# Gates of two of three branches moved from small tiles into halves of weight tiles during the up products of a gated three-branch layer

## The chip, the cores and the metric

One core of a Trainium2 chip runs the whole layer as one program. The metric is the device time of that program in microseconds, the median of three runs. Besides TensorE (PE in the profile) the core has VectorE (DVE), ScalarE (ACT), GpSimd (POOL) and SyncE (SP). In this kernel SP issues almost all transfers from its instruction stream, in order; POOL issues the transfers that add to what is already in a tile.

## The reference, cut to what matters

The input x is 512 tokens by 2048 channels, one layer, all in fp32. What the change touches is the last third of the layer:

```python
hn = rmsnorm(x, norm_g)
proj = einsum('bsd,dc->bsc', hn, w_in)
gates = sigmoid(proj[..., QKVG_COLS + N_HEADS:] + b_gate).reshape(b, s, 3, 2048)
# ya, yb, yc: three attention branches over proj, 4 heads of 128 each
ys = stack([from_heads(ya), from_heads(yb), from_heads(yc)], axis=2)
ys = ys * silu(br[:, :, :, 3])
up = einsum('bsnw,nwd->bsnd', ys, w_up)        # 3 branches, 512 -> 2048
merged = sum(gates * up, axis=2)
return x + einsum('bsd,de->bse', merged, w_out)
```

## The kernel before

**Arithmetic.** Every fp32 product is made of three reduced-precision matmuls: each operand is split into a high and a low half. A weight tile arrives as `raw` (128x1024 fp32, 512 KB, 8 tiles, `NR`); ACT copies it to `wh` (`prep`, L409, 3 buffers), DVE subtracts to get `wl` (L419, 2 buffers), and from then on the raw tile is free. PE runs the products of one such tile, a *unit*, at L277. The input projection and the output product use a seven-product scheme of block sums, for which some `w_out` and `w_in` tiles are first added to each other in DRAM-to-SBUF transfers that POOL issues (`add_up`, L320).

**Stages.** First the input projection and the attention heads (to about 980 us), then the up products, then the output product. The up products go through 12 pairs (g, b): g is one of four quarters of the 2048 output channels, b the branch (0 is C, 1 is B, 2 is A). Their order is `UPS`: (0,0) (0,1) (2,0) (2,1) (0,2) (2,2) (1,0) (1,1) (1,2) (3,0) (3,1) (3,2). A pair has two units of 24 matmuls, and in the second of them its four blocks of 128 tokens (tb) end one after the other. A tile of the output product serves 12 matmuls; the first eight `w_out` tiles are loaded while up products run, and four of them get another tile added first. The attention products of the last A head (L1111 to L1113) stand in the middle of this stage.

**Gates.** The gate logits were stored to DRAM earlier (`gl`). For each (g, b, tb), `gates_of` takes one 128x512 tile of the pool `t2` (20 tiles, `NT`; 3 of them, `KEPT`, are held back from tasks with slack), reads the logits into it (SP, L293, `sg<-gl`), and ACT makes the sigmoid (L1305). `taken` in `up_units` then empties PSUM: DVE multiplies the block by the gate (L1321) and, for b of 1 and 2, adds it to the sum of the branches before it (L1328). After that the tile of b = 1, 2 goes back to `t2`; that of b = 0 holds the sum.

**Merged sums.** When the third branch of a quarter is done, the sum must be turned, channels to partitions. Quarters 0 and 2 go through DRAM: a 32x32 transpose on DVE (L1354), a store, four transposing reads (`back`, L312). Quarters 1 and 3 are turned on PE (`spun_m`, L1385) and copied out by ACT (L1392). Each turned block becomes a *first half* (quarters 0 and 1: one DVE subtraction at L1401, one split at L258 and L262) or a *second half* (quarters 2 and 3: three DVE operations of 128x256 at L268, and three splits).

**What sets the order.** The program is written out by a planner (`Flow`) that keeps a clock for each engine and takes, from the tasks that can start earliest on an engine, the one with the smallest due time: its ready time plus its slack (`MAS` for first halves, `MBS` for second halves), or an explicit one. A task asks the pools (`Slots`) for tiles and waits, in the plan, until one is free. On the chip every engine then follows its written list. A load that stands in SP's list ahead of others holds them up until its own tile is free. Weight loads are issued by one task (`loads`), in the order of the units, as soon as a raw tile is free; gate reads are listed three or two units ahead of the pair's first unit.

Of the kernel before, what the change touches and what calls it, by code (L numbers as in the profile page):

```python
# [21 lines left out]
NB = 3  # L22
# [5 lines left out]
NQ = 4  # L28
# [7 lines left out]
A, B, C = 0, 1, 2  # L36
# [28 lines left out]
class Flow:  # L65
# [16 lines left out]
    def give(self, slots, n=1):  # L82
        slots.free += [self.fin] * n
# [6 lines left out]
    def advance(self, task):  # L90
        while True:
            self.ready = task.ready
            w = task.wait
            if w is None:
                w = next(task.gen, None)
                if w is None:
                    self.tasks.remove(task)
                    task.engine = None
                    return
            task.wait = w  # L100
            if isinstance(w, Event):
                if w.t is None:
                    return
                task.ready = max(task.ready, w.t)
            elif callable(w):
                if not w():
                    return
            elif isinstance(w[0], Slots):
                slots, n = w
                more = n + (slots.kept if task.slack > 1 else 0)  # L110
                if len(slots.free) < more:
                    return
                slots.free.sort()
                due = max(task.ready, slots.free[more - 1])
                if due > self.now + EARLY:
                    task.until = due
                    return
                task.ready = max(task.ready, slots.free[n - 1])
                del slots.free[:n]
            else:  # L120
                task.engine, task.cost = w[:2]
                if task.engine != task.prev:
                    task.ready = max(task.ready, task.fin)
                    if task.engine == PE:
                        task.ready += MARGIN
                task.due = w[2] if len(w) > 2 else task.ready + task.slack
                return
            task.wait = None
# [47 lines left out]
def hybrid_kernel(  # L176
# [30 lines left out]
    flow = Flow()  # L207
# [4 lines left out]
    def t2(s, dt=F32):  # L212
        return tp.tile([P, S], dt, tag="t2", name=nm(s))
# [77 lines left out]
    def fetch(to, src, kb, run=2048):  # L291
        yield issue(0.37)
        nc.sync.dma_start(to, src)  # L293
        return Event(landing(flow.fin, kb, run))
# [82 lines left out]
    def at(u, g, slack=5.0):  # L377
        side.setdefault(u, []).append((g, slack))
# [379 lines left out]
    gl = {}  # L758
# [535 lines left out]

    sig, sig_ev = {}, {}

    def gates_of(n, g, tb):
        if (g, (C, B, A).index(n)) not in UPS[:EARLYG]:
            yield last_head.event("hl", 2)
        yield t2s, 1  # L1300
        t = sig[n, g, tb] = t2("sg")
        yield (yield from fetch(t, gl[n, g, tb], 256))
        yield last_head.event("g")
        yield ACT, act_us(S) + 0.1
        nc.scalar.activation(t, t, AF.Sigmoid)  # L1305
        set_(sig_ev[n, g, tb])

    merged, merged_ev = {}, {}

    def up_units(g, b):  # L1310
        n = (C, B, A)[b]
        ps = [None] * QB
        for tb in range(QB):
            sig_ev[n, g, tb] = Event()
            merged_ev[b, g, tb] = Event()

        def taken(tb):
            yield sig_ev[n, g, tb]
            t = sig[n, g, tb]
            yield DVE, dve_us(S)  # L1320
            nc.vector.tensor_mul(t, ps[tb], t)  # L1321
            give(accs)
            if b == 0:
                merged[g, tb] = t
            else:
                yield merged_ev[b - 1, g, tb]
                yield DVE, dve_us(S)
                nc.vector.tensor_add(merged[g, tb], merged[g, tb], t)  # L1328
                give(t2s)
            set_(merged_ev[b, g, tb])  # L1330

        def mms(i):
            def block(k, tb):
                y = b * NH + 2 * i + k
                return ys[y] and (*ys[y].block(tb), y_ev[y])

            def go(u):
                yield from products(u, ps, (0, 1), range(QB), block, i == 0, i == 1, None if i else (accs, acc),
                                    done=taken, outer=True)
            return go  # L1340

        return [Unit(mms(i), srcs=[w_up[g, b, i]]) for i in range(2)]
# [18 lines left out]
    def turned_m(g, i):  # L1361
        for tb in range(QB):
            yield md_ev[g, tb]
        yield t2s, 1
        m = t2("m")
        ev = yield from back(m, md[g][:, :, blk(i)])
        yield Event(ev.t + MEXTRA)
        arrived(g, i, m)
# [9 lines left out]
    def spun_m(g, i):  # L1378
        for tb in range(QB):
            yield merged_ev[NB - 1, g, tb]  # L1380
        yield atts, 1
        yield PE, 0.11 * QB
        ps = att()
        for tb in range(QB):
            nc.tensor.transpose(ps[:, blk(tb)], merged[g, tb][:, blk(i)], identf)  # L1385
        turns[g] = turns.get(g, 0) + 1
        if turns[g] == QB:
            give(t2s, QB)
        yield t2s, 1
        yield ACT, act_us(S)  # L1390
        m = t2("m")
        nc.scalar.activation(m, ps, AF.Copy)  # L1392
        give(atts)
        arrived(g, i, m)
# [11 lines left out]
    def merged_b(k, b):  # L1406
        a = kept_m[k]
        yield m1_ev[k]
        yield t2s, 1
        t = t2("mt")  # L1410
        if k % 2 == 0:
            yield t2s, 1
            mus[k // 2] = t2("mu")
        u = mus[k // 2][:, RH if k % 2 else LH]
        q = DVE, dve_us(HS)
        yield q
        minus(t[:, LH], b[:, RH], a[:, RH])
        yield q
        minus(t[:, RH], t[:, LH], a[:, LH])
        give(t2s)  # L1420
        yield q
        minus(u, t[:, LH], b[:, LH])
        yield xps, 1
        ev = Event()
        m23[k] = Parts("m23", [ev, ev])
        yield from split(m23[k].hi, m23[k].lo, two(t), S, ev)
        give(t2s)
        if k % 2 == 0:
            yield xps, 1
            m4[k // 2] = Parts("m4")  # L1430
            set_(m4_ev[k // 2])
        yield xps, 1
        ev = Event()
        m2[k] = Parts("m2", [ev, ev])
        yield from split(m2[k].hi, m2[k].lo, two(b), S, ev)
        give(t2s)
        yield m4_ev[k // 2]
        h, lo, ev = m4[k // 2].half(k % 2)
        yield from split(h, lo, u, HS, ev)
        if k % 2:  # L1440
            give(t2s)

    for g, b in UPS:
        for tb in range(QB):
            at(len(units) - (3 - tb // 2 if g or b else 2), lambda n=(C, B, A)[b], g=g, tb=tb: gates_of(n, g, tb))
        units.extend(up_units(g, b))
        if b < NB - 1:
            continue
        for i in range(QB):
            if g in DRAMS:  # L1450
                at(len(units) - 1, lambda g=g, i=i: folded(g, i))
                at(len(units) - 1 + MSKIP, lambda g=g, i=i: turned_m(g, i))
            else:
                at(len(units) - 1, lambda g=g, i=i: spun_m(g, i))
# [34 lines left out]
    def loads():  # L1489
        def x(kt):  # L1490
            yield t2s, 1
            if kt == 0:
                xraw[0], x_in[0].t = x_first, 3.6
                return
            xraw[kt] = t2("x")
            x_in[kt].t = (yield from fetch(xraw[kt], xT[kt], 256)).t

        def n(i):
            n_in[i].t = (yield from fetch(xnat[i // 2][:, i % 2, :], xn[i // NQ, i % NQ], 256)).t

        order = [("x", 0), ("w", 0), ("x", 1), ("w", 1), ("x", 2), ("x", 3), ("w", 2)] + [("n", i) for i in range(4)]
        order += [("x", 4), ("x", 5), ("w", 3)] + [("n", i) for i in range(4, 8)]
        order += [("x", 6), ("x", 7), ("w", 4)] + [("n", i) for i in range(8, 12)]
        order += [("x", 8), ("x", 9), ("w", 5)] + [("n", i) for i in range(12, 14)]
        for i in range(6, 9):
            order += [("x", 2 * i - 2), ("x", 2 * i - 1), ("w", i)] + [("n", j) for j in (14, 15) if i == 7]
        for kind, i in order:
            if kind == "x":
                yield from x(i)
            elif kind == "n":  # L1510
                yield from n(i)
            else:
                yield from units[i].load()
        for u in units[9:]:
            yield from u.load()

    for u, v in zip(units, units[1:]):
# [45 lines left out]
HSLACK = 12.0  # L1563
ENDSLACK, ENDOFF = 3.0, 3
EARLYG = 1
MEXTRA = 4.0
MAS = 1.0
MBS = 3.0

_OUT = (QB, NQ, P, S)  # L1570

# [45 lines left out]
```

## Time and profile before

| | |
|---|---|
| median of 3 runs | 1292.18 us (1288.53 to 1295.38) |
| the profiled execution | 1284.99 us |
| its span (first to last instruction) | 1283.3 us |
| what lies around the span | 1.7 us |
| PE busy | 1272.8 us, 99% of the span |
| DVE busy | 996.6 us, 78% |
| ACT busy | 754.6 us, 59% |
| POOL busy | 91.5 us, 7% |

Times inside the trace count from the start of the span. Three kinds of rows are used below. A row of a timeline has the start, the duration and the number of instructions that were run back to back, and in square brackets the idle time of the engine before it with what ended that. A row of the table by windows has, for each stretch, the busy time of PE, PEld, DVE, ACT and POOL with instruction counts, the granted clock of PE and the busy share and rate of the transfers. A row of the waits has an engine and line, what it waited for, and the total, the number and the longest.

### The profile page before, as it was taken

What the parts mean: (1) busy time and instruction counts of PE and PEld (TensorE: products, weight loads), DVE (VectorE), ACT (ScalarE), POOL (GpSimd) and SP (SyncE); (2) the same over time, 40 slices, a digit from 0 to 9 for tenths busy, and PEclk for the clock granted to TensorE, in tenths of its full rate; (3) what the DMA queues carried; (4) which work ended last, traced back from release to release, by engine and by line L of the source; (5) the groups of instructions that cost most, each with busy time, mean ns of one, the idle gap of its engine ahead of it and who ended that gap; (6) DMA issues with size and microseconds to landing.
All of it is one profiled execution on the core that took longest, in us unless ns stands there. A gap on an engine that the chain in (4) does not pass through costs nothing.

```text
span 1283.3 us, 17347 instructions
## 1 busy us (share of the span) xinstructions
PE 1272.8 (99%) x5716; PEld 1050.5 (82%) x5716; DVE 996.6 (78%) x1398; ACT 754.6 (59%) x1243; POOL 91.5 (7%) x115
## 2 busy tenths in 40 slices
PE   9999999999999999999999999999999999899998
PEld 7788888888888888888888888888887788788887
DVE  6948896987969677697776967769789587897665
ACT  7836566645856667566675666756657543664442
POOL 0001000110110101011011110101100000010100
PEclk9999999999999999999999999999999999999999
DMA  9685799987889878898788987889979979747863
GB/s 357 208 210 123 202 230 225 257 221 200 229 199 252 215 214 235 201 258 215 208 235 202 258 214 208 235 201 260 224 207 350 271 243 212 234 83 236 236 171 129
DMA packets 260666, 284.42 MB, mean 222 GB/s; under 512 B 169808, under 2 KB 180560, under 8 KB 260576
## 3 DMA queue, kind: packets, MB, share of 16 engines
q1 hardware_dynamic: 243152, 224.32, 58.4%
q0 software_dynamic: 14976, 54.53, 22.8%
q10 hardware_dynamic: 2448, 4.46, 0.9%
q8 instruction: 45, 0.74, 0.2%
q14 instruction: 45, 0.37, 0.1%
HBM read 240.73 MB, written 42.51 MB: 221 GB/s over the span
## 4 chain that ended last, share of the span: by engine, by line
PE 91%; DMA 5%; DVE 3%; SPq 1%; issue 1%; ACT 0%; DVEq 0%; ACTq 0%; POOLq 0%
PE acc L277 87%; DMA sg<-gl 1%; DMA raw<-in_w_col 1%; DMA al<-pd 1%; DVE wl L419 1%; PE att L273 1%; PE att L274 1%; PE att L272 1%; PE att L1113 1%; PE att L1112 1%; PE att L1111 1%; DMA raw<-in_w_up 1%; DVE m L262 1%; DMA gl<-v 0%; SPq L293 0%
## 5 line engine op out<-in xcount | busy, mean ns | idle before, releaser
L419 DVE TENSOR_TENSOR wl<-raw,wh 128x1024 fp32r<-128x1024 f32 (+1 forms) x405 | 492.5, 1217 | 227.5 <-PE acc L277 137.3
L409 ACT ACTIVATE wh<-raw 128x1024 fp32r<-128x1024 f32 (+1 forms) x404 | 426.0, 1056 | 354.7 <-PE acc L277 313.3
L277 PE MATMUL acc<-wh,x 128*128 128x512 f32 x1664 | 423.9, 390 | 0.0
L277 PEld LDWEIGHTS acc<-wh,x 128*128 128x128 f32 x1664 | 311.9, 188 | 68.1 <-issue 3.4
L277 PE MATMUL acc<-wh,t 128*128 128x512 f32 x1056 | 275.1, 390 | 0.0
L277 PE MATMUL acc<-wl,x 128*128 128x512 f32 x832 | 232.3, 390 | 0.8 <-DVE wl L419 0.8
L277 PEld LDWEIGHTS acc<-wh,t 128*128 128x128 f32 x1056 | 197.4, 188 | 40.0
L277 PEld LDWEIGHTS acc<-wl,x 128*128 128x128 f32 x832 | 155.7, 188 | 33.6 <-DVE wl L419 1.7
L277 PE MATMUL acc<-wl,t 128*128 128x512 f32 x528 | 154.4, 391 | 0.1
L320 POOL DMA_DIRECT2D raw<-in_w_col x88 | 76.1, 864 | 843.3 <-DMA raw<-in_w_col 228.6
L630 DVE TENSOR_TENSOR raw<-raw,raw 128x1024 f32<-128x1024 f32 x104 | 126.7, 1218 | 0.1
L277 PEld LDWEIGHTS acc<-wl,t 128*128 128x128 f32 x528 | 98.2, 188 | 20.9 <-DVE wl L419 1.2
L277 PE MATMUL acc<-wh,m 128*128 128x512 f32 x448 | 114.5, 389 | 0.0
L277 PE MATMUL acc<-wh,y 128*128 128x512 f32 x384 | 104.3, 393 | 2.2 <-DVE sg L1321 2.2
L277 PEld LDWEIGHTS acc<-wh,m 128*128 128x128 f32 x448 | 84.0, 188 | 17.5
L277 PEld LDWEIGHTS acc<-wh,y 128*128 128x128 f32 x384 | 72.5, 189 | 17.7 <-DVE sg L1321 2.6
L277 PE MATMUL acc<-wl,m 128*128 128x512 f32 x224 | 63.6, 390 | 0.2 <-DVE wl L419 0.2
L277 PE MATMUL acc<-wl,y 128*128 128x512 f32 x192 | 60.6, 395 | 0.0
L714 ACT ACTIVATE u<-acc 128x512 f32<-128x512 f32 x52 | 31.1, 598 | 41.4 <-PE acc L277 40.2
L277 PEld LDWEIGHTS acc<-wl,m 128*128 128x128 f32 x224 | 41.9, 188 | 9.2 <-DVE wl L419 0.6
L1321 DVE TENSOR_TENSOR sg<-acc,sg 128x512 f32<-128x512 f32 x48 | 32.7, 687 | 13.1 <-ACT sg L1305 8.3
L1305 ACT ACTIVATE sg<-sg 128x512 f32<-128x512 f32 x48 | 28.1, 621 | 24.7 <-DMA sg<-gl 24.6
(155 smaller groups left out, 960.9 us busy)
## 6 DMA issues: line engine op xcount, KB each, us to landing
raw<-in_w_col SPq DMA_DIRECT2D x191, 512.0 KB, 4.9
raw<-in_w_col POOLq DMA_DIRECT2D x88, 512.0 KB, 8.2
raw<-in_w_out SPq DMA_DIRECT2D x32, 512.0 KB, 4.0
raw<-in_w_up SPq DMA_DIRECT2D x24, 512.0 KB, 5.7
sg<-gl SPq DMA_DIRECT2D x48, 256.0 KB, 4.9
gl<-u SPq DMA_DIRECT2D x44, 256.0 KB, 4.7
raw<-in_w_out POOLq DMA_DIRECT2D x16, 512.0 KB, 6.3
qkl<-qd SPq DMA_DIRECT2D x96, 64.0 KB, 4.1
```

The costliest lines, as they stand in the source:

```text
L262: nc.vector.tensor_sub(lo, src, f(hi))
L272: nc.tensor.matmul(ps, lh, rh, start=start, stop=False, skip_group_check=more)
L273: nc.tensor.matmul(ps, lh, rl, start=False, stop=False, skip_group_check=more)
L274: nc.tensor.matmul(ps, ll, rh, start=False, stop=stop, skip_group_check=more)
L277: nc.tensor.matmul(ps, w, x, start=start, stop=stop, skip_group_check=more)
L320: nc.gpsimd.dma_start(to, src, accum_op=ALU.add)
L409: nc.scalar.activation(u.hi, u.raw, AF.Copy)
L419: nc.vector.tensor_sub(u.lo, u.raw, f(u.hi))
L630: nc.vector.tensor_add(to.raw, to.raw, self.raw)
L714: nc.scalar.activation(t, w, AF.Copy)
L1305: nc.scalar.activation(t, t, AF.Sigmoid)
L1321: nc.vector.tensor_mul(t, ps[tb], t)
```

## The change

**Gates of branches 1 and 2 no longer use `t2`.** A new pool `pairs` is filled with four of the eight raw tiles (`NPAIR`) at the point in `loads` where the first up unit's weight would be loaded. Two token blocks of a gate share one such tile, one half each; when both blocks have been added to the sum, the tile returns to `pairs`, and the last four go back to the weights. Between these points four raw tiles are left for `w_up` and for the first `w_out` tiles. Gates of branch 0 still take `t2` tiles, and the tiles of the merged sums (`m`, `mt`, `mu`) may now use the three that were held back.

**Order.** Gate reads are listed one unit earlier (`GAHEAD`), the plan counts each gate's data as there 4 us later (`GEXTRA`), the transposing reads 7 instead of 4 us later (`MEXTRA`), and first and second halves have slacks of 4 and 10 us instead of 1 and 3 (`MAS`, `MBS`). The lines after the new code move: L1305 is L1317, L1321 is L1346, L1328 is L1353, L1354 is L1379, L1385 is L1410, L1392 is L1417 and L1401 is L1426.

No matrix product, sigmoid, multiplication or transfer is added or left out. All four compute lists are the same up to about the end of the attention heads.

The core of the diff:

```diff
-                more = n + (slots.kept if task.slack > 1 else 0)
+                more = n + (slots.kept if task.slack > 1 and len(w) < 3 else 0)
...
+    pairs = Slots(0)
+
     def gates_of(n, g, tb):
         if (g, (C, B, A).index(n)) not in UPS[:EARLYG]:
             yield last_head.event("hl", 2)
-        yield t2s, 1
-        t = sig[n, g, tb] = t2("sg")
-        yield (yield from fetch(t, gl[n, g, tb], 256))
+        if n == C:
+            yield t2s, 1
+            t = sig[n, g, tb] = t2("sg")
+        else:
+            if tb % 2 == 0:
+                yield pairs, 1
+                both = raw_tile()
+                sig[n, g, tb], sig[n, g, tb + 1] = both[:, 0, :], both[:, 1, :]
+                set_(pair_ev[n, g, tb // 2])
+            yield pair_ev[n, g, tb // 2]
+            t = sig[n, g, tb]
+        ev = yield from fetch(t, gl[n, g, tb], 256)
+        yield Event(ev.t + GEXTRA)
         yield last_head.event("g")
         yield ACT, act_us(S) + 0.1
         nc.scalar.activation(t, t, AF.Sigmoid)
         set_(sig_ev[n, g, tb])
...
+    def pair_used(n, g, h):
+        pair_n[n, g, h] = pair_n.get((n, g, h), 0) + 1
+        if pair_n[n, g, h] == 2:
+            give(pairs)
+            pair_n["all"] = pair_n.get("all", 0) + 1
+            if pair_n["all"] > 2 * NQ * (NB - 1) - NPAIR:
+                pairs.free.sort()
+                raws.free.append(pairs.free.pop())
...
                 nc.vector.tensor_add(merged[g, tb], merged[g, tb], t)
-                give(t2s)
+                pair_used(n, g, tb // 2)
...
-        yield t2s, 1
+        yield t2s, 1, True
         m = t2("m")
...
-            at(len(units) - (3 - tb // 2 if g or b else 2), lambda n=(C, B, A)[b], g=g, tb=tb: gates_of(n, g, tb))
+            at(len(units) - (3 - tb // 2 + GAHEAD if g or b else 2), lambda n=(C, B, A)[b], g=g, tb=tb: gates_of(n, g, tb))
...
-        for u in units[9:]:
+        for i, u in enumerate(units[9:]):
+            if i + 9 == end:
+                yield raws, NPAIR
+                pairs.free += [max(flow.ready, flow.now)] * NPAIR
             yield from u.load()
...
-MEXTRA = 4.0
-MAS = 1.0
-MBS = 3.0
+MEXTRA = 7.0
+MAS = 4.0
+MBS = 10.0
+GEXTRA = 4.0
+GAHEAD = 1
+NPAIR = 4
```

Below, `order` rows show a stretch of one engine's list: the line, the instruction, the tile written and the tiles read, each with the number of its allocation, and the shape. First SP's list where the last gates of quarter 3 and the first `w_out` tiles are read, before (the logits `gl` numbered 3676 to 3840 are those of branch 0, 6519 to 6677 of branch 1):

```order
L293 DMA raw_9781<-in_w_out 128x1024
L293 DMA sg_9792<-gl_3698 128x512
L293 DMA sg_9807<-gl_3821 128x512
L293 DMA raw_9860<-in_w_out 128x1024
L293 DMA raw_9892<-in_w_out 128x1024
L293 DMA sg_9899<-gl_3840 128x512
L293 DMA raw_9942<-in_w_out 128x1024
L293 DMA sg_10008<-gl_6519 128x512
L293 DMA sg_10009<-gl_6541 128x512
L293 DMA raw_10017<-in_w_out 128x1024
```

and in the changed kernel (8937 to 8863 are of branch 2):

```order
L293 DMA raw_9712<-gl_6519 128x512
L293 DMA raw_9712<-gl_6541 128x512
L293 DMA raw_9734<-in_w_up 128x1024
```

with, eight transposing reads further down:

```order
L293 DMA raw_9771<-in_w_up 128x1024
L293 DMA raw_9760<-gl_6654 128x512
L293 DMA raw_9760<-gl_6677 128x512
L293 DMA raw_9805<-gl_8937 128x512
L293 DMA raw_9805<-gl_8944 128x512
L293 DMA raw_9829<-in_w_up 128x1024
L293 DMA raw_9881<-gl_8857 128x512
L293 DMA raw_9881<-gl_8863 128x512
L293 DMA raw_9897<-in_w_out 128x1024
L293 DMA raw_9964<-in_w_out 128x1024
```

Before, loads of `w_out` stood between the gate reads; now every gate read stands ahead of the first of them, with loads of `w_up` between.

Second, DVE's list at the end of pair (3,1), whose PSUM blocks are emptied by the rows with `acc`, before:

```order
L1401 TENSOR_TENSOR m_10040<-m_10040 128x256
L262 TENSOR_TENSOR m_1753_10044<-m_10034,m_1753_10044 128x2x256
L268 SCALAR_TENSOR_TENSOR mt_10010<-mt_10010,m_9570 128x256
L262 TENSOR_TENSOR m_1755_10056<-m_10040,m_1755_10056 128x2x256
L262 TENSOR_TENSOR m_1721_9915<-mu_9869,m_1721_9915 128x256
L419 TENSOR_TENSOR wl_10060<-raw_9646,wh_9987 128x1024
L262 TENSOR_TENSOR m_1742_9994<-mu_9946,m_1742_9994 128x256
L1321 TENSOR_TENSOR sg_10008<-acc_9925,sg_10008 128x512
L268 SCALAR_TENSOR_TENSOR mu_9946<-mt_10010,m_9737 128x256
L1321 TENSOR_TENSOR sg_10009<-acc_9938,sg_10009 128x512
L1328 TENSOR_TENSOR sg_9675<-sg_9675,sg_10008 128x512
L1328 TENSOR_TENSOR sg_9792<-sg_9792,sg_10009 128x512
```

and now:

```order
L419 TENSOR_TENSOR wl_9995<-raw_9771,wh_9939 128x1024
L1346 TENSOR_TENSOR raw_9712<-acc_9940,raw_9712 128x512
L1353 TENSOR_TENSOR sg_9613<-sg_9613,raw_9712 128x512
L1346 TENSOR_TENSOR raw_9712<-acc_9956,raw_9712 128x512
L1353 TENSOR_TENSOR sg_9614<-sg_9614,raw_9712 128x512
L1346 TENSOR_TENSOR raw_9760<-acc_9967,raw_9760 128x512
L1353 TENSOR_TENSOR sg_9660<-sg_9660,raw_9760 128x512
L268 SCALAR_TENSOR_TENSOR mt_9951<-mt_9951,m_9554 128x256
L1346 TENSOR_TENSOR raw_9760<-acc_9978,raw_9760 128x512
L1353 TENSOR_TENSOR sg_9661<-sg_9661,raw_9760 128x512
```

The first emptying of this pair stood behind first and second halves (L1401, L268, L262) of the merged sums; now it stands behind the weight's low half, and the four follow each other with one operation of a second half between.

Third, ACT's list near the start of the up products, where the four gates of pair (0,1) are made. The weights there are those of the sixth (`wh_9098`) and the seventh up unit (`wh_9137`), and the gates are the four after and around them, before:

```order
L409 ACTIVATE wh_9098<-raw_8863 128x1024
L1305 ACTIVATE sg_9018<-sg_9018 128x512
L1305 ACTIVATE sg_9026<-sg_9026 128x512
L1305 ACTIVATE sg_9045<-sg_9045 128x512
L409 ACTIVATE wh_9137<-raw_8897 128x1024
L1305 ACTIVATE sg_9064<-sg_9064 128x512
```

and now, where `wh_9094` is the sixth unit's and `wh_9132` the seventh's:

```order
L1317 ACTIVATE sg_8904<-sg_8904 128x512
L1317 ACTIVATE sg_8913<-sg_8913 128x512
L1317 ACTIVATE sg_8919<-sg_8919 128x512
L409 ACTIVATE wh_9094<-raw_8957 128x1024
L409 ACTIVATE wh_9132<-raw_9014 128x1024
L1317 ACTIVATE raw_8990<-raw_8990 128x512 x2
L1317 ACTIVATE raw_8991<-raw_8991 128x512 x2
```

Three of the four gates stood behind the sixth unit's weight and one behind the seventh's; now all four stand behind the seventh's.

More of the change, by code (lines that the diff above doesn't have):

```diff
@@ L108, in advance @@
             elif isinstance(w[0], Slots):
-                slots, n = w
-                more = n + (slots.kept if task.slack > 1 else 0)
+                slots, n = w[:2]
+                more = n + (slots.kept if task.slack > 1 and len(w) < 3 else 0)
                 if len(slots.free) < more:
@@ L1306, in gates_of @@
         set_(sig_ev[n, g, tb])
+    pair_ev, pair_n = {}, {}
+    def pair_used(n, g, h):
[6 more added lines that the diff above has]
+                raws.free.append(pairs.free.pop())
     merged, merged_ev = {}, {}
@@ L1312, in up_units @@
         ps = [None] * QB
+        for h in range(2):
+            pair_ev[n, g, h] = Event()
         for tb in range(QB):
@@ L1388, in spun_m @@
             give(t2s, QB)
-        yield t2s, 1
+        yield t2s, 1, True
         yield ACT, act_us(S)
@@ L1408, in merged_b @@
         yield m1_ev[k]
-        yield t2s, 1
+        yield t2s, 1, True
         t = t2("mt")
         if k % 2 == 0:
-            yield t2s, 1
+            yield t2s, 1, True
             mus[k // 2] = t2("mu")
```

## The prediction, made before the changed kernel was run

> **What bounds the kernel now.** I read the page first: the busy shares, the chain, the costliest groups.
>
> ```profile
> span 1283.3 us, 17347 instructions
> PE 1272.8 (99%) x5716; PEld 1050.5 (82%) x5716; DVE 996.6 (78%) x1398; ACT 754.6 (59%) x1243; POOL 91.5 (7%) x115
> L409 ACT ACTIVATE wh<-raw 128x1024 fp32r<-128x1024 f32 (+1 forms) x404 | 426.0, 1056 | 354.7 <-PE acc L277 313.3
> L419 DVE TENSOR_TENSOR wl<-raw,wh 128x1024 fp32r<-128x1024 f32 (+1 forms) x405 | 492.5, 1217 | 227.5 <-PE acc L277 137.3
> L1321 DVE TENSOR_TENSOR sg<-acc,sg 128x512 f32<-128x512 f32 x48 | 32.7, 687 | 13.1 <-ACT sg L1305 8.3
> L1305 ACT ACTIVATE sg<-sg 128x512 f32<-128x512 f32 x48 | 28.1, 621 | 24.7 <-DMA sg<-gl 24.6
> ```
>
> PE is the bound. It is outside its 1272.8 busy microseconds for 10.5 us in all, and the change adds or removes no matmul, so it can win only time that PE loses in the up products, and lose what it breaks there. So the second view is the table by windows of ten microseconds through that stage, and the third the waits of PE.
>
> ```profile
> 1000.00:1010.00 10.00, 10.00 (x46) 8.28 (x45) 6.54 (x10) 3.67 (x6) 0.00 (x0) 1.00 0.86 234
> 1010.00:1020.00 10.00, 9.18 (x43) 7.18 (x42) 6.78 (x12) 6.07 (x11) 0.00 (x0) 1.00 1.00 369
> 1100.00:1110.00 10.00, 8.48 (x41) 6.50 (x40) 10.00 (x21) 7.59 (x15) 1.72 (x2) 1.00 0.72 192
> 1110.00:1120.00 10.00, 7.78 (x27) 5.97 (x26) 10.00 (x19) 6.74 (x12) 0.00 (x0) 0.83 0.93 283
> ```
> ```profile
> PE acc L277 <- DVE sg L1321: 2.2, 1, 2.2
> PE att L1385 <- ACT m L1392: 1.5, 2, 1.0
> ```
>
> In an ordinary window PE is busy for all 10 us (second column). Three windows are not: one near 1010 and the last two of the stage, where DVE is busy for every microsecond (10.00) and the granted clock falls to 0.83. The timeline of PE shows each place:
>
> ```profile
> 982.84 1.07 PE L277 MATMUL acc<-wh,y 128*128 128x512 f32 x4
> 1012.48 0.39 PE L277 MATMUL acc<-wl,y 128*128 128x512 f32 x1
> 1013.68 0.50 PE L1111 MATMUL att<-ah,vh 128*128 128x512 f32 x1 [0.82 <-ACT ah L258]
> 1014.75 0.39 PE L277 MATMUL acc<-wl,y 128*128 128x512 f32 x1
> 1101.65 0.66 PE L1385 MATMUL att<-identf,sg 128*128 128x128 f32 x4 [0.49 <-ACT m L1392]
> 1104.72 0.66 PE L1385 MATMUL att<-identf,sg 128*128 128x128 f32 x4 [1.02 <-ACT m L1392]
> 1107.06 1.07 PE L277 MATMUL acc<-wh,y 128*128 128x512 f32 x4
> 1108.42 1.07 PE L277 MATMUL acc<-wh,y 128*128 128x512 f32 x4
> 1114.88 1.39 PE L277 MATMUL acc<-wh,y 128*128 128x512 f32 x4 [2.22 <-DVE sg L1321]
> 1119.33 1.09 PE L277 MATMUL acc<-wh,y 128*128 128x512 f32 x4
> 1124.81 1.52 PE L277 MATMUL acc<-wh,m 128*128 128x512 f32 x6
> ```
>
> From 1107.06 to 1108.42 four high and two low matmuls take 1.36 us, 0.227 each: the undisturbed pace. The up stage runs from 982.84 to the first output product at 1124.81, 141.97 us. Its 24 units of 24 matmuls take 96 x 1.36 = 130.6 us at that pace; the sixteen transposes of quarter 1 (L1385) and the twelve attention matmuls add about 3.5 us (an estimate from the same pace by their widths, with 0.1 us at least for each). So 7.9 us are lost, and the marks in square brackets say where.
>
> Why the large stall at 1114.88? It waits for an emptying of PSUM (L1321). The timelines of SP, ACT and DVE ahead of it:
>
> ```profile
> 1092.21 0.63 SPq L293 DMA_DIRECT2D sg<-gl  x1
> 1101.90 0.33 SPq L293 DMA_DIRECT2D raw<-in_w_out  x1
> 1102.32 1.57 SPq L293 DMA_DIRECT2D sg<-gl  x2
> 1107.53 0.33 SPq L293 DMA_DIRECT2D raw<-in_w_out  x1
> 1107.95 2.00 SPq L293 DMA_DIRECT2D sg<-gl  x4
> ```
> ```profile
> 1112.40 1.13 ACT L1305 ACTIVATE sg<-sg 128x512 f32<-128x512 f32 x2
> 1113.96 1.13 ACT L1305 ACTIVATE sg<-sg 128x512 f32<-128x512 f32 x2
> ```
> ```profile
> 1112.66 1.22 DVE L419 TENSOR_TENSOR wl<-raw,wh 128x1024 fp32r<-128x1024 f32 x1
> 1114.13 0.69 DVE L1321 TENSOR_TENSOR sg<-acc,sg 128x512 f32<-128x512 f32 x1
> ```
>
> SP stands still from 1092.8 to 1101.9: a load of `w_out` waits for its tile, and two gate reads are issued only behind it, at 1102.32, then again four at 1107.95. Their sigmoids are made at 1112.40 and 1113.96, and DVE, which works through merged halves without a gap, comes to the emptying at 1114.13. Two things hold PE there together: gates read late, and halves listed ahead of the emptying.
>
> **The change, part by part.** *Gates in raw halves, a unit earlier.* In the new list all gate reads stand ahead of the first `w_out` load, and what they wait for is the adds of an earlier pair. The last pairs' gates then lie ready many microseconds ahead, and the sigmoids cannot be late near 1112. The read itself costs what it did.
>
> *Slack of the halves.* In the new DVE list the four emptyings of (3,1) follow the weight's low half, with one operation of a second half among them. What was ahead of them (in the rows shown, six operations of L1401, L262 and L268) comes later, beside output products. DVE is idle for 4.67 us of the stretch below, and each low half of a `w_out` tile there takes 1.22 us against 12 matmuls or 2.72 us of PE, so the moved work has cover; without it each operation would be 0.42 or 0.69 us of PE wait.
>
> ```profile
> 1090.00:1100.00 10.00, 10.00 (x50) 8.37 (x49) 5.33 (x10) 3.88 (x7) 0.00 (x0) 1.00 0.98 289
> ```
>
> Terms, all against the profiled execution:
> 1. The wait of 2.22 us at 1114.88 goes.
> 2. So does the slow stretch behind it. From 1114.88 to 1119.33 PE runs twelve matmuls, 2.72 us at the usual pace, in 4.45: 1.73 us, and the window shows the clock at 0.83.
> 3. The transposes of quarter 1 waited 0.49 and 1.02 us for ACT's copies, which were queued behind splits of halves. In the new list they directly follow pair (1,2) and eight of sixteen run at once: 1.51 us saved. Their copies now share ACT with sigmoids, and by the durations (0.58 a copy) I find 0.4 to 1.1 us of room.
> 4. At 1013.68 the attention product waited for `ah` on ACT. From 1012.48 to 1014.75 one up matmul and three attention matmuls took 2.27 us, 0.91 at pace: 1.36 us lost. ACT's list before had `ah` behind sigmoids whose data had not come:
>
> ```profile
> 1011.83 1.28 ACT L1305 ACTIVATE sg<-sg 128x512 f32<-128x512 f32 x2 [2.76 <-DMA sg<-gl]
> 1013.02 0.61 ACT L258 ACTIVATE ah<-al 128x512 fp32r<-128x512 f32 x1
> ```
>
> In the new list `ah` stands ahead of the next weight, and the product stands about 4 us later on PE. 1.36 us saved.
>
> The sum is 2.22 + 1.73 + 1.51 + 1.36 = 6.82 us. About 1.1 us of the 7.9 are in no row that I can name; part may go too. On the other side stand waits of a few tenths where the room is small. I take 6.8: 1284.99 - 6.8 = 1278.2 for the profiled execution. That execution is 7.2 us below the median of the runs; the same saving from the median gives 1292.18 - 6.8 = 1285.4. Bounds of the saving where the mechanism holds: 5.3 (term 4 or 3 stays) to 7.9.
>
> On term 2 the Trainium skill, "TensorE: Matmul & The Clock Gate", section "Why this matters for your kernels", asks only that no gap be longer than about 3 us, since one idle window drops the clock. The gap here is 2.22 us, and the clock dropped all the same, so the trace speaks against the bound.
>
> *Four raw tiles.* A `w_up` load now waits for the low half four units back, about 3 x 5.44 = 16 us ahead of its use by ACT; a load takes 5.8 us to landing, so it is hidden. The first `w_out` loads are another matter: before, the last stood at 1113.92 and the fourth add at 1108.61; now loads come 12 to 17 us later.
>
> ```profile
> raw<-in_w_out SPq DMA_DIRECT2D x8, 512.0 KB, 5.9
> raw<-in_w_up SPq DMA_DIRECT2D x18, 512.0 KB, 5.8
> raw<-in_w_out POOLq DMA_DIRECT2D x4, 512.0 KB, 6.9
> 1108.61 0.86 POOL L320 DMA_DIRECT2D raw<-in_w_out  x1 [7.28 <-ACT m L1392]
> ```
>
> The tightest is the fifth. Its tile is free after the last add of (3,1). With the output at 1118.0, the two last units start at 1107.1 and 1112.6, so that add ends near 1107.1 + 2 x 0.69 = 1108.5; the load lands at 1114.4, the adding transfer 0.86 + 6.9 later, at 1122.2. PE needs the tile after four output units, 1118.0 + 4 x 2.72 = 1128.9 (plus transposes), and ACT and DVE need 1.06 + 1.22 before: 1126.6. Room 4.4 us, so I count nothing.
>
> **The rivals.**
> *A. New short waits eat half.* All four gates of (0,1) now stand behind the seventh unit's weight, which needs a `wh` buffer that the fourth unit frees at 982.84 + 4 x 5.44 = 1004.6. Weight 1.06, sigmoid 0.62, emptying 0.69: PSUM comes free at 1006.97, and PE wants it about two blocks into the fifth unit, 1004.6 + 2.72 = 1007.3. A room of 0.35 us. Before, three of the four stood a unit earlier, and the window from 1000 shows no loss. If any of these comes 1 us late, PE waits 1 us, and waits with a slower clock behind them cost nearly double (2.22 became 3.95). With a second such place, at the transposes' copies, 3.5 us go: saving 3.3, that is 1288.9, within 0.5% (6.46 us of 1292.18, about what a measurement of this kernel can tell from no change). For it: the small room. Against it: DMA and DVE have free time there (0.86, 6.54 of 10).
>
> *B. The stall only moves.* DVE is full from 1100 to 1120. If the work that is taken from ahead of the emptyings is not covered further on, output products wait for halves instead, for the same 2.22 + 1.73, and only terms 3 and 4 stay: saving 2.9, 1289.3. Against it: in the 20 us before, DVE had idle time, and first halves now come earlier.
>
> *C. Slower: too few weight tiles.* If the late `w_out` loads and their adds meet the gate reads and the output's first units wait for them, each wait is like the one at 1114.88, 3.95 us with its slow stretch. The four adds come in a row, one output unit each; four such waits are 15.8 us, less 6.8 gained: 9.0 slower, 1301.2. It decides where load and add together take 13.7 + 4.4 = 18.1 us. Against it: the rows have 5.9 and 6.9, and the transfers are busy 0.72 and 0.93 there, not more.
>
> *D. No effect.* If the planner's gates come early but DVE's and ACT's real pace puts other work there, all four terms could remain, 1292.
>
> *E. The slow stretch is not the stall's.* If the 1.73 us behind 1114.88 have another cause, they stay: saving 6.82 - 1.73 = 5.1, 1287.1. Against it: of the four windows shown, only the one with the stall has a clock below 1.00. It is what the skill's page named above would have for a gap of this length. 0.05.
>
> **How the numbers follow.** Forecast 0.55: saving 5.3 to 7.9 around 6.8, of which four fifths lie over 6.46. A 0.2, B 0.07, E 0.05, D 0.05, C 0.08. Faster by over 0.5%: 0.44. Slower: C 0.08, and a little from D with unfriendly waits, 0.1. Between: 0.46. The range: the runs before spread by 3.4 us to either side of the median, which the forecast's lower bound takes on (1292.18 - 7.9 - 3.4 = 1280.9, I write 1280); above it reaches over A, B and E to 1289.3, and with the same 3.4 to 1292.7. C is left out.
>
> **What would show it.** Right: no wait on L1346 behind DVE near 1110, the window there at 10.00 busy and clock 1.00; transposes in a block without brackets; the first `ah` product without a wait; the first output product near 1118.0 in the span instead of 1124.81; first emptying of (0,1) done by 1007. Wrong: PE waits at the fifth to seventh unit (A), on `wh` or `wl` of `w_out` or halves after 1118 (B, C), SP waiting for tiles ahead of gate reads as now (D). If the first output product comes at 1118 and the end is not 6.8 us earlier, the loss is in the output stage.

## The result and the profile after

The changed kernel takes 1279.26 us in the median of 11 runs (1276.48 to 1283.82), the kernel before 1287.03 us in the median of 11 (1284.30 to 1295.38). The ratio is 0.9936, 95% interval 0.9915 to 0.9956: 8.2 us less by the middle, 5.7 to 10.9 by the interval. The direction was right and the forecast saving of 6.8 us lies within this interval, but the time came out 0.74 us below the low end of the stated range, 1280.0. The profiled execution took 1277.93 us with a span of 1276.2, against 1284.99 and 1283.3: 7.1 us less.

First the page of the changed kernel, then its table by windows, and all that PE waited for in the whole execution. In all fences below, `...` stands for rows left out.

```profile
span 1276.2 us, 17343 instructions
PE 1269.5 (99%) x5716; PEld 1049.3 (82%) x5716; DVE 997.0 (78%) x1398; ACT 753.5 (59%) x1243; POOL 91.6 (7%) x115
```
```profile
1000.00:1010.00 10.00, 10.00 (x46) 8.29 (x45) 5.28 (x7) 5.62 (x9) 0.00 (x0) 1.00 0.91 273
1010.00:1020.00 10.00, 10.00 (x46) 8.37 (x45) 8.52 (x14) 7.60 (x15) 0.00 (x0) 1.00 1.07 335
1100.00:1110.00 10.00, 10.00 (x46) 8.29 (x45) 9.76 (x19) 5.23 (x9) 1.72 (x2) 1.00 0.81 213
1110.00:1120.00 10.00, 10.00 (x46) 8.29 (x45) 9.90 (x16) 4.18 (x7) 1.73 (x2) 1.00 0.81 233
```
```profile
PE att L467 <- DVE mskf L341: 1.1, 1, 1.1
PE acc L277 <- DVE wh L406: 0.7, 1, 0.7
PE acc L277 <- ACT wh L409: 0.6, 1, 0.6
PE acc L277 <- DVE wl L419: 0.5, 2, 0.3
```

The three windows that lost time are full and at clock 1.00; no wait on an emptying, a transpose's copy or `ah` is left. DVE is still nearly full there (9.76 and 9.90): what changed is not how much it does but in which order. The timeline of PE at the places of the prediction:

```profile
981.91 0.74 PE L277 MATMUL acc<-wl,t 128*128 128x512 f32 x2 [0.23 <-DVE wl L419]
983.89 1.08 PE L277 MATMUL acc<-wh,y 128*128 128x512 f32 x4
...
1017.44 0.39 PE L1111 MATMUL att<-ah,vh 128*128 128x512 f32 x1
...
1086.04 1.03 PE L1410 MATMUL att<-identf,sg 128*128 128x128 f32 x8
...
1118.25 1.98 PE L277 MATMUL acc<-wh,m 128*128 128x512 f32 x8
```

The up stage, from the first up product to the first output product, takes 1118.25 - 983.89 = 134.36 us, where it took 141.97: 7.61 less, and the 134.1 that PE needs at its pace (130.6 and 3.5) is reached within 0.3. The output stage took 157.95 us after 158.49, 0.54 less. Against that the up stage starts 1.05 us later. Sum: -7.61 - 0.54 + 1.05 = -7.1.

SP, ACT and DVE ahead of the place where PE stalled for 2.22 us:

```profile
1091.54 1.80 SPq L293 DMA_DIRECT2D raw<-gl  x4
1093.44 0.40 SPq L293 DMA_DIRECT2D raw<-in_w_up  x1
1093.93 0.97 SPq L293 DMA_DIRECT2D raw<-gl  x2
1095.29 25.97 SPq L293 DMA_DIRECT2D raw<-in_w_out  x8
```
```profile
1096.94 1.66 ACT L1317 ACTIVATE raw<-raw 128x512 f32<-128x512 f32 x3
...
1100.04 1.30 ACT L1317 ACTIVATE raw<-raw 128x512 f32<-128x512 f32 x2
```
```profile
1103.06 1.22 DVE L419 TENSOR_TENSOR wl<-raw,wh 128x1024 fp32r<-128x1024 f32 x1
1104.19 0.68 DVE L1346 TENSOR_TENSOR raw<-acc,raw 128x512 f32<-128x512 f32 x1
```

The last gate read is issued by 1094.9, the eight `w_out` loads hang behind it for 26 us and hold up no gate; all sigmoids of the stage are done by 1101.34, while in the kernel before those at 1112.40 and 1113.96 were still to come; and the emptying of (3,1) begins at 1104.19 instead of 1114.13.

### The profile page after: what moved, and what is told of

The parts are those of the page before. It is cut to its first block, busy times and chain, and to the rows that moved or that the text cites. A ratio compares the mean times of both kernels' runs of the same rounds, so it can differ in the third digit from the quotient of the medians.

```text
span 1276.2 us, 17343 instructions
## 1 busy us (share of the span) xinstructions
PE 1269.5 (99%) x5716; PEld 1049.3 (82%) x5716; DVE 997.0 (78%) x1398; ACT 753.5 (59%) x1243; POOL 91.6 (7%) x115
## 4 chain that ended last, share of the span: by engine, by line
PE 97%; DMA 2%; DVE 1%; SPq 0%; ACT 0%; issue 0%; DVEq 0%
PE acc L277 93%; DMA raw<-in_w_col 1%; PE att L1112 1%; PE att L1113 1%; PE att L274 1%; PE att L273 1%; PE att L272 1%; DMA raw<-in_w_up 1%; PE att L1111 1%; DVE wl L419 0%; PE att L778 0%; DMA x<-in_xT 0%; PE att L1410 0%; DVE u L1162 0%; DVE p L992 0%
## 5 line engine op out<-in xcount | busy, mean ns | idle before, releaser
L419 DVE TENSOR_TENSOR wl<-raw,wh 128x1024 fp32r<-128x1024 f32 (+1 forms) x405 | 492.2, 1216 | 224.9 <-PE acc L277 140.1
L277 PEld LDWEIGHTS acc<-wl,y 128*128 128x128 f32 x192 | 35.9, 188 | 7.3
L320 POOL DMA_DIRECT2D raw<-in_w_out x16 | 13.8, 863 | 277.6 <-ACT m L258 177.5
```

The source lines that it names most:

```text
L277: nc.tensor.matmul(ps, w, x, start=start, stop=stop, skip_group_check=more)
L320: nc.gpsimd.dma_start(to, src, accum_op=ALU.add)
L419: nc.vector.tensor_sub(u.lo, u.raw, f(u.hi))
```

## The experiments

The measure in most of them is the up stage, since its length can be read to a few hundredths of a microsecond. Each length is that of one profiled execution, and in the kernel before it differs from one execution to the next (e13 to e16 below: 138.5 to 143.3). First product and first output product of each run, in us; the last column is the median where a kernel was timed several times, else the single time:

| kernel | starts | ends | length | time |
|---|---|---|---|---|
| before | 982.84 | 1124.81 | 141.97 | 1287.03 |
| changed | 983.89 | 1118.25 | 134.36 | 1279.26 |
| e1, slack of second halves alone | 982.22 | 1123.41 | 141.19 | 1284.00 |
| e2, gates in raw halves alone | 983.67 | 1122.80 | 139.13 | 1284.33 |
| e3, and read ahead | 984.01 | 1118.37 | 134.36 | 1279.64 |
| e4, raw halves and slack | 982.21 | 1117.29 | 135.08 | 1279.42 |
| e5, low half 9 dummies late | 991.24 | 1125.61 | 134.37 | 1285.30 |
| e6, 11 dummies | 984.18 | 1119.52 | 135.34 | 1279.18 |
| e9, 12 dummies | 983.36 | 1119.16 | 135.80 | 1278.81 |
| e10, 13 dummies | 983.74 | 1119.97 | 136.23 | 1279.64 |
| e7, 14 dummies | 983.83 | 1122.13 | 138.30 | 1281.81 |
| e8, two weight tiles | 987.14 | 1128.25 | 141.11 | 1292.13 |
| e11, reserve in halves | 982.56 | 1117.09 | 134.53 | 1279.43 |
| e12, reserve late | 986.44 | 1120.80 | 134.36 | 1278.24 |

### Which part of the change does it

**e1.** In the kernel before:

```diff
-MBS = 3.0
+MBS = 10.0
```

> The kernel before with one edit: second halves of the merged sums get a slack of 10 us instead of 3 in the plan; gates stay in the small tiles and are read as late as before. Measure: the up stage, from the first up product to the first output product, 141.97 us before and 134.36 after the change. Theory (late gate reads and halves listed ahead of the emptyings hold PE together, so either alone leaves most of the loss): the attention wait and the late sigmoids stay, up stage 138 to 142 us, total within 0.3% of before. Rival (the order of the halves alone was the cause): the large stall and its slow stretch go, up stage about 137 or less, total 4 to 5 us less than before.

Ratio 0.9972 (0.9958 to 0.9986), up stage 141.19 us. The waits of PE, and its timeline at the worst of them:

```profile
PE att L1385 <- ACT m L1392: 3.1, 2, 1.9
```
```profile
1105.87 0.65 PE L1385 MATMUL att<-identf,sg 128*128 128x128 f32 x4 [1.92 <-ACT m L1392]
1106.28 1.03 PE L277 MATMUL acc<-wl,y 128*128 128x512 f32 x2
1107.11 1.91 PE L277 MATMUL acc<-wh,y 128*128 128x512 f32 x4
1108.82 1.06 PE L277 MATMUL acc<-wl,y 128*128 128x512 f32 x2
1109.67 1.20 PE L277 MATMUL acc<-wh,y 128*128 128x512 f32 x4
```

The wait on an emptying is gone as the new order says, but a transpose waits 1.92 us for its copy instead, and the slow stretch moved behind that wait: eight matmuls from 1106.28 to 1109.67 in 3.39 us instead of 1.81. So the stall only moves, as in rival B, though to a transpose in the same stage and not to output products, and it is the slack without the tiles that does it. By all runs the gain is 0.28% or 3.6 us, by the one profiled up stage 0.8; the repeats at the end of this section show that executions of one kernel differ by that much, so the stage of one profile does not size this gain. The theory's bounds (138 to 142 us, within 0.3%) held.

**e2 and e3.** In the changed kernel, e2 with

```diff
-MEXTRA = 7.0
-MAS = 4.0
-MBS = 10.0
-GEXTRA = 4.0
-GAHEAD = 1
+MEXTRA = 4.0
+MAS = 1.0
+MBS = 3.0
+GEXTRA = 0.0
+GAHEAD = 0
```

and e3 with the first three of these only.

> The changed kernel with gates in raw halves, but reads listed as in before (no unit earlier, no 4 us in the plan) and the old slacks and transposing-read allowance. Theory: gate reads no longer stand between the w_out loads, the emptyings still stand behind halves; the wait on an emptying shrinks but stays, up stage 136 to 140 us. Rival (gate tiles alone are the cause): up stage 135 or less, all of the gain. Rival (order of halves alone): up stage as before, 141 to 142.

> The changed kernel with the old slacks (1 and 3 us) and allowance (4 us), gates in raw halves and read a unit earlier. Theory: sigmoids are never late, but DVE comes to emptyings of quarter 3 behind first and second halves; PE waits there about 1 us or more with a slow stretch, up stage 135.5 to 138 us, total 2 to 5 us above the changed kernel. Rival (gates read late were the whole cause): no PE wait on an emptying, up stage 134.4, total as the changed kernel.

e2: ratio 0.9982 (0.9966 to 0.9998), up stage 139.13 us, 2.8 less than in the one profile of before but inside the 138.5 to 143.3 of its repeats. The emptyings no longer stall PE, the copies do:

```profile
1096.67 1.01 PE L1410 MATMUL att<-identf,sg 128*128 128x128 f32 x4 [2.32 <-ACT m L1417]
```
```profile
1093.00 0.63 ACT L1317 ACTIVATE raw<-raw 128x512 f32<-128x512 f32 x1 [6.26 <-DMA raw<-gl]
1093.54 1.04 ACT L409 ACTIVATE wh<-raw 128x1024 fp32r<-128x1024 f32 x1
1094.48 1.65 ACT L1317 ACTIVATE raw<-raw 128x512 f32<-128x512 f32 x3
1096.04 1.06 ACT L1417 ACTIVATE m<-att 128x512 f32<-128x512 f32 x2
```

ACT stands idle for 6.26 us in front of a gate that has not landed, and a weight, three sigmoids and the copies for which PE waits are queued behind it. e3: ratio 0.9938 (0.9916 to 0.9960), 134.36 us, the whole gain, with short slacks and emptyings between halves. The expectation of the theory (1 us of wait or more) was wrong, the rival's right: with the gates there in time, the old order of the halves costs nothing.

**e4.** The changed kernel with

```diff
-GEXTRA = 4.0
-GAHEAD = 1
+GEXTRA = 0.0
+GAHEAD = 0
```

> The changed kernel with gates in raw halves and the new slacks, but reads listed as late as in before and no 4 us in the plan. Theory: with the emptyings ahead of the halves and the reads out of the way of the w_out loads, at most the attention wait returns (1.4 us): up stage 134.4 to 136.5 us. Rival (a unit earlier is what matters): sigmoids wait for data, PE waits at several emptyings, up stage 138 or more.

Ratio 0.9944 (0.9922 to 0.9966), up stage 135.08 us: 6.9 of the 7.6 us. The only wait that PE shows for a gate is 0.2 us at an attention product. So on top of the new tiles either the earlier read or the slack is enough, or nearly so; without them the slack leaves transposes waiting for 3.1 us (e1). Two parts were not tried alone: reads a unit earlier within the small tiles, and the three held-back tiles for the merged sums, which e2, e3 and e4 all have.

### What a wait costs

The dummies in e5 to e7, e9 and e10 are multiplications of the raw weight by 1.0 ahead of one low half (`prep` of the 16th up unit), k of them:

```diff
         yield DVE, dve_us(n)
+        for _ in range(k if u is units[end + 15] else 0):
+            nc.vector.tensor_scalar(u.raw[:, 0, :], u.raw[:, 0, :], 1.0, 0.0, op0=ALU.mult, op1=ALU.add)
         nc.vector.tensor_sub(u.lo, u.raw, f(u.hi))
```

> The changed kernel with nine dummy DVE operations of 128x512 (0.60 us each, 5.4 us) ahead of the low half of the weight of the 16th up unit, which has about 4.4 us of room: one PE wait of about 1.0 us there, nothing else. Theory (the slow stretch is the stall's): the cost of the wait is its own length, since the waits of 0.49 and 1.02 us before were followed by matmuls at the usual pace. Rival: a wait of any length costs nearly double, about 2 us from the wait's start to the usual pace.

> The same with eleven dummies (6.6 us): one PE wait of about 2.2 us, as long as the stall of the kernel before, but in the middle of the stage, with DVE not full and no output loads near. Theory: the granted clock drops behind it and the next matmuls lose about 1.7 us more, as at 1114.88 before. Rival (the slow stretch had another cause; this is also what the page 'TensorE: Matmul & The Clock Gate' would have, with its limit of about 3 us): the clock stays at 1.00 and only 2.2 us are lost.

> The changed kernel with twelve dummy DVE operations ahead of the low half of the 16th up unit's weight. Eleven gave a wait of 0.65 us with the clock at 1.00 behind it, fourteen one of 2.03 us with 0.83; twelve should give 0.65 + 0.60 = 1.25 us. Theory (the wait of 1.02 us before was followed by the usual pace): usual pace behind it, up stage 134.36 + 1.6 = 136.0 us. Rival (any wait over a microsecond slows the clock): 1.6 us more.

> The same with thirteen dummies: a wait of about 1.6 to 1.9 us. If the slow stretch comes with it, up stage about 137.9 us and a clock below 1.00 behind it; if not, 136.3 us. No theory here says which; it narrows where the slow stretch begins.

> The same with fourteen dummies (8.4 us): one PE wait of about 4.0 us. Theory: the same slow stretch behind it, about 1.7 us, perhaps more. Rival: with a slow stretch only here and not at 2.2 us, the limit lies between.

A dummy costs 0.46 us and not 0.60 (fourteen ran back to back in 6.42 us; waits of 0.65, 1.11, 1.58 and 2.03 us for 11 to 14), so nine gave no wait and the others less than expected. PE behind thirteen and behind fourteen:

```profile
1069.95 0.73 PE L277 MATMUL acc<-wl,y 128*128 128x512 f32 x2 [1.58 <-DVE wl L421]
1070.52 1.08 PE L277 MATMUL acc<-wh,y 128*128 128x512 f32 x4
1071.44 0.61 PE L277 MATMUL acc<-wl,y 128*128 128x512 f32 x2
```
```profile
1070.49 0.73 PE L277 MATMUL acc<-wl,y 128*128 128x512 f32 x2 [2.03 <-DVE wl L421]
1071.06 1.15 PE L277 MATMUL acc<-wh,y 128*128 128x512 f32 x4
1072.00 1.06 PE L277 MATMUL acc<-wl,y 128*128 128x512 f32 x2
1072.85 1.91 PE L277 MATMUL acc<-wh,y 128*128 128x512 f32 x4
1074.56 1.00 PE L277 MATMUL acc<-wl,y 128*128 128x512 f32 x2
1075.40 1.08 PE L277 MATMUL acc<-wh,y 128*128 128x512 f32 x4
```

Behind 1.58 us four high matmuls take 0.92 us, the usual pace; behind 2.03 us they take 1.71 at 1072.85, and twelve matmuls 4.34 us instead of 2.72: 1.62 lost, after 1.73 at 1114.88 in the kernel before. The stages tell the same: 0.46, 0.43, then 2.07 us for one more dummy. So the slow stretch follows from the wait, in the middle of the stage too, with no output load near. Rival E is refuted. The limit of about 3 us in the Trainium skill, "TensorE: Matmul & The Clock Gate", section "Why this matters for your kernels", is too high for this kernel: 1.92, 2.03 and 2.22 us were followed by it.

### Few weight tiles

**e8.** The changed kernel with `NPAIR = 6`.

> The changed kernel with six raw tiles set aside for gates instead of four, so two are left for weights in the up stage. Theory (four tiles had room of 4 to 6 us at the first output loads, a load and its adding transfer take about 13.7 us): with two, a load waits for the low half two units back, 16 instead of 27 us ahead of its product; up products still run, the first output products wait for their loads or adds: 5 to 15 us slower than the changed kernel. Rival (loads are hidden anyway): within 1 us of the changed kernel.

Ratio 1.0044 (1.0020 to 1.0068) to the kernel before, 1292.13 us: slower by about 13 us than the changed kernel, as the theory said, but not where it said. Where PE waited:

```profile
987.14 1.19 PE L277 MATMUL acc<-wh,y 128*128 128x512 f32 x4 [3.50 <-ACT wh L409]
...
1102.32 0.66 PE L1410 MATMUL att<-identf,sg 128*128 128x128 f32 x4 [2.05 <-ACT m L1417]
1102.73 0.70 PE L277 MATMUL acc<-wh,y 128*128 128x512 f32 x2
```

The first up product waits 3.50 us for a weight that was loaded only when six tiles were free, and ACT's copies wait behind a late weight near 1102. The output stage takes 1286.3 - 1128.25 = 158.05 us, as in the changed kernel: even with two tiles no output product waits for its load. Rival C had the right resource and the wrong place. And the wait of 2.05 us is followed by the usual pace, while one of 2.03 in e7 is not: near 2 us, length alone does not decide.

The clock records of the traces show what does. The granted clock changes only in steps of 3.413 us: in the kernel before it is halved from 1115.72 to 1119.13 and changes next 163.84 us later, which is 48 steps; in e1 the next change comes 50 steps later, in e7 60, in e8 86. Cut into stretches of one step, the waits of e7 and of e8 look like this (behind each stretch stand its length and PE's busy time, third from the end the clock):

```profile
1068.54:1071.95 3.41, 1.46 (x6) 1.24 (x7) 3.34 (x5) 0.70 (x2) 0.00 (x0) 1.00 0.19 25
1071.95:1075.36 3.41, 3.41 (x9) 2.67 (x8) 2.30 (x4) 0.00 (x0) 0.00 (x0) 0.50 0.99 321
```
```profile
1097.75:1101.16 3.41, 2.52 (x12) 1.75 (x10) 2.04 (x4) 1.48 (x3) 0.00 (x0) 1.00 1.01 398
1101.16:1104.57 3.41, 2.25 (x12) 1.95 (x13) 2.76 (x5) 3.41 (x6) 0.00 (x0) 1.00 1.04 414
1104.57:1107.98 3.41, 3.41 (x17) 2.81 (x16) 3.41 (x8) 3.41 (x7) 0.00 (x0) 1.00 0.94 363
```

In e7 nearly all of the wait lies in one stretch, 1.95 us idle, and the next stretch runs at half the clock. In e8 the wait falls on a boundary, 0.89 and 1.16 us, and the clock stays; so does one of 2.15 us in e16 below, 0.97 and 1.18. Over all the traces here, a full-clock stretch with 1.92 us or more of idle PE is always followed by one at half the clock, and one with 1.5 us or less never; the two between went either way (1.76 us in e15 without, 1.56 us in e12, in the input projection, with). A stretch at half the clock loses half of its 3.41 us, 1.7, which is the 1.73 and 1.62 us above.

### The later start

**e11 and e12.** Four tiles are set aside in two steps (e11), or three units later (e12):

```diff
-            if i + 9 == end:
-                yield raws, NPAIR
-                pairs.free += [max(flow.ready, flow.now)] * NPAIR
+            if i + 9 in (end, end + 2):
+                yield raws, NPAIR // 2
+                pairs.free += [max(flow.ready, flow.now)] * (NPAIR // 2)
```
```diff
-            if i + 9 == end:
+            if i + 9 == end + 3:
```

> The changed kernel with two raw tiles set aside for gates at the first up unit and two more two units later, so six are left for weights across the entry to the up stage. Theory (the entry lost about 0.5 us to weight loads that came late because four tiles were held): the wait ahead of the first up product (0.23 us shown, 0.4 in all) goes or shrinks, first up product about 0.5 us earlier, up stage as the changed kernel, total 0 to 0.6 us less. Rival: the held tiles do not matter at the entry, no difference.

> The changed kernel with the four raw tiles set aside three units later. Theory: the entry runs as in the kernel before (no wait ahead of the first up product); gates of (0,1) come a little later, and since two of them have about 0.4 us of room by the list, PE may wait up to 1 us at the fifth unit; total within 1 us of the changed kernel. Rival (rival A of the prediction, small rooms eat the gain): a wait with a slow stretch, 3 us or more above the changed kernel.

e11: ratio 0.9944 (0.9925 to 0.9962), up stage 134.53; e12: 0.9934 (0.9908 to 0.9960), 134.36. Neither can be told from the changed kernel in time. DVE and PE tell why one starts without a wait. In e11 DVE makes one half of `y` (L262) between two low halves (L419):

```profile
978.64 0.68 DVE L262 TENSOR_TENSOR y<-yr,y 128x512 fp32r<-128x512 f32 x1
```

and in e12, as in the changed kernel, two, so that the second low half begins 2.34 us after the first (980.85 and 983.19) and not 1.73 (977.51 and 979.24 in e11):

```profile
981.98 1.29 DVE L262 TENSOR_TENSOR y<-yr,y 128x512 fp32r<-128x512 f32 x2
```

The 0.5 us lost at the entry (in the changed kernel 4.32 us from the four low matmuls at 979.57 to the first up product at 983.89, in e11 3.78) go with one more `y` operation ahead of a low half; the kernel before and e1 have one there and no wait. This is read from the traces: no run moved that operation alone. The theory that tiles held back are late there has fallen: e12 loads its first weights early and has nearly the same wait (0.20 us after 0.23).

### What the kernel before does from run to run

**e13 to e16** profile the unchanged kernel before again.

> The kernel before, unchanged, profiled again. Theory (the runs of before spread from 1280 to 1295 by single late weight loads in the input projection, as one profiled execution of another kernel here lost about 6.6 us at 744 us; the up stage itself repeats): up stage 141.5 to 142.5 us in each execution, span differing by the start of the up stage alone, at 980 to 992 us. Rival (the stall at the end of the up stage varies from run to run, so the saving does): up stages between 138 and 146.

> As the run before it: the kernel before, unchanged, a third execution.

> As the run before it: the kernel before, unchanged, a fourth execution.

> As the run before it: the kernel before, unchanged, a fifth execution.

The times are 1288.15, 1285.04, 1285.74 and 1289.47 us. Up stages: 142.65, 138.52, 139.30 and 143.28, so with the first profile 138.5 to 143.3, mean 141.1. Starts: 985.36, 986.37, 986.25 and 986.03, after 982.84. The first two of them at the stall:

```profile
1118.12 1.31 PE L277 MATMUL acc<-wh,y 128*128 128x512 f32 x4 [2.21 <-DVE sg L1321]
...
1128.01 1.98 PE L277 MATMUL acc<-wh,m 128*128 128x512 f32 x8
```
```profile
1116.60 1.20 PE L277 MATMUL acc<-wh,y 128*128 128x512 f32 x4 [0.91 <-DVE sg L1321]
...
1124.89 1.98 PE L277 MATMUL acc<-wh,m 128*128 128x512 f32 x8
```

In two of the five executions (e14, e15) the stall is 0.91 us, the clock stays at 1.00 and the stage takes about 139 us; in three the stall is 2.2, the clock is halved once and the stage takes 142 to 143. Which of the two happens is not explained here. The wait of the attention product for `ah` is 0.82 to 2.15 us. The theory (the stage repeats) was wrong, the rival right: the saving itself is a matter of the execution, 4.2 to 8.9 us. In the changed kernel and those that stall nowhere (e3, e5, e12) the stage is 134.36 to 134.37 each time. What else differs lies ahead of the stage: e5 took 1285.30 us although its up stage is as short as any, since one weight of the input projection came late:

```profile
744.28 2.08 PE L277 MATMUL acc<-wh,t 128*128 128x512 f32 x4 [4.05 <-ACT wh L409]
```

From there twelve matmuls take until 749.57, 5.29 us instead of 2.72, with the clock halved from 743.16 to 749.98, so this one wait costs 6.6 us. Why that transfer was late in this execution is open.

## Why the prediction was right and wrong

**The base of the range failed.** The saving was well sized: 6.82 by the sum, 7.1 in the spans, 6.8 against the mean of five up stages of before (141.14 - 134.36). But the step "the runs before spread by 3.4 us to either side of the median" counted the low end from 1292.18, the median of three runs, all three slower than each of the eight that came with the changed kernel. The median of the 11 is 1287.03. The profiled execution at 1284.99, below all three, already stood in the text and was set aside with "the same saving from the median". Weighing it in (mean of the four 1290.3) would have given 1290.3 - 7.9 - 3.4 = 1279.0, which holds the time, though that is hindsight. Nor were the three a fair sample: of 59 later runs of this kernel, in four sets, none reaches 1292.18 (the highest is 1291.90), and the medians of the three later sets are 1286.77, 1286.17 and 1286.98. Why the first three came out so high is open.

**Terms 1 and 2** (2.22 and 1.73 us) went, as forecast. They were taken from one execution of five; in two others the stall was 0.91 us with no slow stretch. So the size of these terms depends on the execution: in e14 the same reckoning would have found 138.52 - 134.1 = 4.4 us to win instead of 7.9. That the profile at hand lay near the mean of the five was luck. The slow stretch itself was rightly laid to the stall (e7).

**Term 3** (1.51 us): right, no bracket at 1086.04. Its cause was put down to halves ahead of the copies alone; e2 shows gates that have not landed doing the same.

**Term 4** (1.36 us): right, the product at 1017.44 has no wait.

**"Two things hold PE there together"**: too much. Given the new tiles, the earlier read removes it all (e3) and the slack nearly all (e4), so these two can stand in for each other. Tiles alone and slack alone do not suffice: by the runs they gain 0.18% and 0.28% where the whole change gains 0.64%, and their up stages lie within the spread of the kernel before.

**What was counted at nothing.** The emptying of (0,1), rival A, ended at 1007.74, 2.1 us into the fifth unit, where 2.72 were allowed: it held. The output loads held too. Not foreseen were 0.5 us at the entry, from DVE's order there, and 0.54 us won in the output stage.

**The rivals.** A did not happen. B did not happen either; a stall that only moves appears in e1, at a transpose. C's resource is real and appears in e8, at the entry and the copies, not at the output. D did not happen. E is refuted by e7.

## What to carry to other kernels

A load that waits for its tile in an in-order issue list delays everything listed behind it; it pays to list the small early reads ahead of the large prefetch, which takes a tile of their own for them. Judge a stall by the time to the next full-pace product, not by the wait alone; here the same wait cost 1.7 us more or not, by how it fell on the steps of the clock. And before a saving of half a per cent is set against a base, take every execution of the base, the profiled one too, and look whether the stall itself repeats.

## What the runs showed of the hardware

The granted clock changed only at steps of 3.413 us, and a step with 1.92 us or more of idle PE was followed by one at half the clock, in which a matmul took 0.43 us instead of 0.227. So waits of PE of 1.92, 2.03, 2.20 to 2.22, 2.32, 3.50 and 4.05 us were followed by a slow stretch, and those of 2.05 (e8) and 2.15 us (e16), which fell on the boundary of two steps, were not. Waits of up to 1.76 us in the up stage left the pace as it was; one of 1.50 us in the input projection of e12 did not. A wait just over 2 us thus cost 3.9 us in the stage (138.30 against 134.36), one of 1.58 us 1.9.
